# The last modulation row of a mixture-of-experts layer: from the experts' loop to the final sums

## The chip, the cores and the metric

One Trainium2 core runs the whole program. The time is in device microseconds; lower is better. The kernel before took 1674.91 us, the median of three runs (1671.81 to 1677.38). The core's engines work side by side and each takes its instructions in order: TensorE (PE; PEld is its weight load), VectorE (DVE), ScalarE (ACT), GpSimd (POOL), and SyncE (SP), which here only issues transfers.

## The reference

One layer of a diffusion trunk: modulated normalisation, three kinds of attention, an output projection, then a mixture of experts. The change lies in the last two lines of the layer and in the final normalisation.

```python
def hybrid_layer(...):
    mod = (c_act @ w_mod + b_mod).reshape(B_, 6, 1, D)
    ...
    h2 = rms_norm(x, g2) * (1 + mod[:, 4]) + mod[:, 3]
    ...
    f = hier_moe(h2.reshape(-1, D), w_rg, b_rg, w_re, b_re, w_up, w_down)
    x = x + mod[:, 5] * f.reshape(B_, S, D)
    return x, xc

def hier_moe(h, ...):            # top-1 group of 4, top-2 of its 8 experts: 32 experts
    gate = jax.nn.softmax(top_v, axis=-1) * p_grp
    ...
    def expert_block(args):
        g, u = jnp.split(xb @ w_up[e], 2, axis=-1)
        return (jax.nn.silu(g) * u) @ w_down[e]
    y = y[dest] * gate.reshape(-1)[order][:, None].astype(h.dtype)
    return jax.ops.segment_sum(y, tok_sorted, num_segments=n_tok)

def reference(...):
    return rms_norm(x, final_g)
```

There are 1024 tokens of width 1024, all in fp32. Each token goes to two experts; its two results are weighted by two gates, summed, multiplied by the modulation row `mod[5]` (one value for each column, the same for all tokens) and added to `x`.

## The kernel before

The first 940 us (modulation, projections, attention, output projection, routing) are the same in both kernels. Then comes a loop over the 32 experts, written out in full, with 128 places (partitions) for the tokens of each. Tokens beyond 128 for an expert go to overflow blocks in a loop whose count is read from the data (line 1985); in the profiled execution it has no turn.

**The experts' loop.** The weights come in tiles of 128 rows by 1024 columns, eight for an expert's `w_up` and four for its `w_down`, in one stream of 384 (lines 1881 to 1901). They lie in a ring of 34 buffers (`wraw`); SyncE issues the load of tile j + 34 when tile j is split. To multiply in fp32 precision with a faster format, each tile is split in two parts (line 1828): ScalarE rounds it to `whi`, VectorE subtracts to get the remainder `wlo` (line 1832). There are three buffers of each. The tokens are split in the same way into `xh`, `xl`, and the hidden activations into `ah`, `al`. For each tile TensorE does six matmuls of 512 columns (lines 1857 to 1859): high by high, high by low, low by high, for two halves of the columns. The order on the engines is the order in which the code is written (a manual schedule): the `w_up` tiles of expert e + 1 stand ahead of the `w_down` tiles of expert e, and the transposes of tokens and activations are set into the stream.

When the fourth `w_down` tile of an expert is done, `e_scatter` (line 1871) takes the result `py` from PSUM: ScalarE copies it to `y`, GpSimd multiplies `y` by `m5`, the modulation row spread over all partitions (line 1877), and GpSimd issues an indirect transfer that writes the 128 rows to the DRAM table `YS` (line 1878), at row `j * T + token` for choice j. For the last expert alone VectorE does copy and multiplication in one instruction (line 1874). During some seven experts, from (b, k) = (8, 0) on, the overflow tables are built by many small VectorE instructions, one of them behind each step of the stream.

**Behind the loop.** Each of the eight token tiles (128 tokens by 1024) needs its `x` (kept in DRAM as `X1`, loaded into the ring: four by GpSimd behind the scatter of expert 29, four and the final gain `fg` by SyncE), and the two rows of `YS`, `y0` and `y1`, 16 loads of 512 KB issued by SyncE once all scatters have landed. `FINAL` (line 58) is a string that sets the order of the steps `f_step` (line 2016): `s` does x + gate0 y0 + gate1 y1 in two VectorE instructions, `t` gives the first product to ScalarE and the first addition to GpSimd; both end with a ScalarE pass that squares and sums each row. `r` is a chain of small VectorE instructions for 1/sqrt; `o` scales by that and by `fg` on VectorE, `u` does so on ScalarE and GpSimd; both store the tile. This part is ordered by a scheduler that starts from the written order.

Of the kernel before, what the change touches and what calls it, by code (L numbers as in the profile page):

```python
# [8 lines left out]
F32 = mybir.dt.float32  # L9
# [3 lines left out]
AF = mybir.ActivationFunctionType  # L13
OP = mybir.AluOpType
# [4 lines left out]
D = 1024  # L19
# [27 lines left out]
DRAIN = 30  # L47
LATE = 3
HL = 1
XE = 4  # L50
START = """
Lx.0.4 Lm.0 Lx.4.8 R.0 Lm.1 Lw q.3 q.2 q.1 C.0 q.0 x.0.4 w q.5 q.6 q.7 q.4 h.0.0 x.4.8 a.0.0
R.1 h.1.0 Lx.8.10 C.1 q.9 h.2.0 h.3.1 Lm.2 R.2 q.8 h.0.1 h.1.1 x.8.10 Lm.3 C.2 h.2.1 h.3.0 a.1.0 a.0.1 h.1.2
# [1 line left out]
S.3.2 a.4.0 h.6.0 a.5.0 h.7.0 a.4.2 a.1.2 h.7.1 a.2.2 a.6.0 a.7.0 h.6.2 h.5.2 a.6.1 h.7.2 S.3.3 S.3.6 S.3.5 a.3.2 a.7.1  # L55
a.5.1 a.5.2 N a.7.2 a.6.2 S.3.7 a.0.2
"""
FINAL = "t2 s0 s1 r01 o0 t3 o1 r23 t4 t5 o2 r45 t7 t6 o4 u5 r6 r7 o7 o3 o6"
LAST = """
s0.30 T0.28 table.3 m.29 s1.30 x1.30 T4.28 p2.5 T8.28 T0.29 x0.30 v.28 s0.31 T4.29 s1.31 m.30 x0.31 T8.29 router.4  # L60
choose.4 p3.5 mixt.6 v.29 norm2.5 T0.30 T8.30 x1.31 m.31 T4.30 v.30 p0.6 na.7 rank.4 T0.31 T4.31 T8.31 h0.5 h1.5 p1.6
# [6 lines left out]
def body(nc, tc, d, tap=None, upto=None):  # L68
# [7 lines left out]
    def dmab(t, src):  # L76
        nc.sync.dma_start(t, src)  # L77
# [1174 lines left out]
    def ring():  # L1252
        rws.append(rws.pop(0))
        return rws[-1].tile([128, D], F32, name="wraw")
# [616 lines left out]
    def e_scatter(py, si_, last=False):  # L1871
        y = e2.tile([128, D], F32, name="y", bufs=2)
        if last:
            nc.vector.tensor_mul(y, py, m5)
        else:
            nc.scalar.copy(y, py)  # L1876
            nc.gpsimd.tensor_mul(y, y, m5)  # L1877
        return nc.gpsimd.indirect_dma_start(out=YS, out_offset=bass.IndirectOffsetOnAxis(ap=si_, axis=0),
                                            in_=y, in_offset=None, bounds_check=2 * T - 1, oob_is_err=False)

# [19 lines left out]
                load_tile(j + RW)  # L1900


    xts = []

    def load_ends():

        for t in range(XE):
            load_x1(t, nc.gpsimd)

    def load_x1(t, eng):  # L1910
        x2 = ring()
        rws.pop()
        eng.dma_start(x2, X1[t * 128:(t + 1) * 128, :])
        xts.append(x2)

    with tc.manual_schedule(engines={ET.PE, ET.DVE, ET.Activation, ET.Pool}):
# [29 lines left out]
        for j, (b, k) in enumerate(stream):  # L1946
# [20 lines left out]
            if kind == 1 and k == 3:  # L1967
                i_ = e_scatter(ps, sU[:, e:e + 1], e == E - 1)
                for p_ in scat:
                    tc.declare_no_dep(i_.ins, p_.ins, reason="rows of other tokens or choices")  # L1970
                scat.append(i_)
                if e == E - 3:
                    load_ends()
        for _ in side_work:
            pass

    for t in range(XE, NT):
        load_x1(t, nc.sync)
    fg = ring()
    rws.pop()  # L1980
    dmab(fg, bcast_rows(d["final_g"], D))


    nov = nc.values_load(novt[0:1, 0:1], min_val=0, max_val=NOV)
# [27 lines left out]
            dmab(yts[t][j], YS[j * T + t * 128:j * T + (t + 1) * 128, :])  # L2012
    s3 = e2.tile([128, NT], F32, name="s3", bufs=1)
    r3 = e2.tile([128, 2, NT], F32, name="r3", bufs=1)

    def f_step(what, ts):
        t = ts[0]
        xt, y0, y1 = xts[t], *yts[t]
        a, b = ts[0], ts[-1] + 1
        if what == "s":  # L2020
            nc.vector.scalar_tensor_tensor(xt, y0, gate[:, 0, t:t + 1], xt, op0=OP.mult, op1=OP.add)  # L2021
        elif what == "t":
            nc.scalar.activation(y0, y0, AF.Copy, scale=gate[:, 0, t:t + 1])  # L2023
            nc.gpsimd.tensor_add(xt, xt, y0)  # L2024
        if what in "st":
            nc.vector.scalar_tensor_tensor(xt, y1, gate[:, 1, t:t + 1], xt, op0=OP.mult, op1=OP.add)  # L2026
            nc.scalar.activation(y0, xt, AF.Square, accum_out=s3[:, t:t + 1])  # L2027
        elif what == "r":
            nc.vector.tensor_scalar(s3[:, a:b], s3[:, a:b], 1.0 / D, EPS, op0=OP.mult, op1=OP.add)  # L2029
            rsqrt(s3[:, a:b], r3[:, 0, a:b], r3[:, 1, a:b])  # L2030
        elif what == "o":
            nc.vector.scalar_tensor_tensor(xt, xt, r3[:, 0, t:t + 1], fg, op0=OP.mult, op1=OP.mult)  # L2032
        elif what == "u":
            nc.scalar.activation(xt, xt, AF.Copy, scale=r3[:, 0, t:t + 1])
            nc.gpsimd.tensor_mul(xt, xt, fg)
        if what in "ou":
            nc.sync.dma_start(d["out"][t * 128:(t + 1) * 128, :], xt)
# [129 lines left out]
```

## Time and profile before

| what | us |
|---|---|
| median of three runs | 1674.91 |
| the profiled execution, its own time | 1675.7 |
| its span, first to last instruction | 1673.9 |
| first scatter of the loop | at 992.73 |
| last scatter of the loop | at 1615.27 |
| first load of `YS` issued | at 1619.42 |
| last VectorE instruction ends | at 1668.70 |
| PE, DVE, ACT, POOL busy over the span | 1462.1, 1233.5, 999.1, 546.2 |

In a timeline row stand the start, the time, the engine, the line, the operation, what it writes and reads, how many such instructions in a row were put together, and in brackets how long the engine had stood still before it and what ended that. In a row of windows stand the stretch, its length, the busy time of PE, PEld, DVE, ACT and POOL with their instruction counts, the granted clock of TensorE (1 is full speed), the busy share of the 16 DMA engines, and what they moved in GB/s. A wait row names who waited, for whom, the total, how often, and the longest.

### The profile page before, as it was taken

What the parts mean: (1) busy time and instruction counts of PE and PEld (TensorE: products, weight loads), DVE (VectorE), ACT (ScalarE), POOL (GpSimd) and SP (SyncE); (2) the same over time, 40 slices, a digit from 0 to 9 for tenths busy, and PEclk for the clock granted to TensorE, in tenths of its full rate; (3) what the DMA queues carried; (4) which work ended last, traced back from release to release, by engine and by line L of the source; (5) the groups of instructions that cost most, each with busy time, mean ns of one, the idle gap of its engine ahead of it and who ended that gap; (6) DMA issues with size and microseconds to landing.
All of it is one profiled execution on the core that took longest, in us unless ns stands there. A gap on an engine that the chain in (4) does not pass through costs nothing. (4 is left out here: it accounts for less than half of the span.)

```text
span 1673.9 us, 24624 instructions
## 1 busy us (share of the span) xinstructions
PE 1462.1 (87%) x8611; PEld 1193.7 (71%) x8611; DVE 1233.5 (74%) x1936; ACT 999.1 (60%) x1602; POOL 546.2 (33%) x608
## 2 busy tenths in 40 slices
PE   6899799899989897999998689988999999999840
PEld 2698677777777776899998567666777777777730
DVE  5713657965544365867787689998999999999957
ACT  4624546754434523767664377766777777777742
POOL 0201423222322203377885413322222223233224
PEclk9999899999988897999999799999999999999975
DMA  9324572106543686222227789887999999999344
GB/s 325 102 58 137 163 227 67 49 27 186 128 109 96 200 268 244 77 65 89 64 89 273 274 302 337 317 306 261 335 349 344 342 343 344 339 347 340 144 179 192
DMA packets 163502, 353.18 MB, mean 211 GB/s; under 512 B 28247, under 2 KB 83735, under 8 KB 163376
## 3 DMA queue, kind: packets, MB, share of 16 engines
q1 hardware_dynamic: 139552, 307.87, 53.4%
q0 software_dynamic: 22096, 37.94, 7.4%
q10 hardware_dynamic: 1728, 5.78, 0.9%
q8 instruction: 69, 1.13, 0.3%
q14 instruction: 57, 0.47, 0.1%
HBM read 318.30 MB, written 49.30 MB: 220 GB/s over the span
## 5 line engine op out<-in xcount | busy, mean ns | idle before, releaser
L1832 DVE TENSOR_TENSOR wlo<-wraw,whi 128x1024 fp32r<-128x1024 f32 x384 | 505.8, 1338 | 42.8 <-ACT whi L1831 37.7
L1831 ACT CAST whi<-wraw 128x1024 fp32r<-128x1024 f32 x384 | 399.5, 1049 | 160.7 <-PE epu L1859 110.3
L1858 PE MATMUL epu<-wlo,xh 128*128 128x512 f32 x512 | 210.4, 411 | 44.0 <-DVE wlo L1832 42.7
L1857 PE MATMUL epu<-whi,xh 128*128 128x512 f32 x512 | 208.4, 407 | 2.2 <-ACT xh L1849 2.2
L1859 PE MATMUL epu<-whi,xl 128*128 128x512 f32 x512 | 203.9, 398 | 1.0 <-DVE xl L1850 1.0
L1858 PEld LDWEIGHTS epu<-wlo,xh 128*128 128x128 f32 x512 | 97.1, 190 | 89.5 <-DVE wlo L1832 69.3
L1836 POOL DMA_INDIRECT xg<-H,gidx x30 | 42.2, 1407 | 332.2 <-PE ept L1847 320.6
L1877 POOL TENSOR_TENSOR y<-y,m 128x1024 f32<-128x1024 f32 x31 | 88.8, 2865 | 136.2 <-ACT y L1876 136.2
L1273 DVE TENSOR_REDUCE nm<-S 128x1 f32<-128x1280 f32 x64 | 94.9, 1489 | 51.0 <-PE S L1272 42.4
L385 PE MATMUL pj<-wh,hh 128*128 128x256 f32 (+1 forms) x384 | 114.8, 299 | 1.3 <-ACT kbT L342 1.3
L1857 PEld LDWEIGHTS epu<-whi,xh 128*128 128x128 f32 x512 | 97.4, 190 | 24.0 <-ACT xh L1849 2.8
L387 PE MATMUL pj<-wh,hl 128*128 128x256 f32 (+1 forms) x384 | 113.3, 295 | 0.0
L386 PE MATMUL pj<-wl,hh 128*128 128x256 f32 (+1 forms) x384 | 113.3, 295 | 0.0
L1859 PEld LDWEIGHTS epu<-whi,xl 128*128 128x128 f32 x512 | 97.3, 190 | 22.3 <-DVE xl L1850 1.7
L1857 PE MATMUL epy<-whi,ah 128*128 128x512 f32 x256 | 109.0, 426 | 2.3 <-ACT y L1876 2.3
L1858 PE MATMUL epy<-wlo,ah 128*128 128x512 f32 x256 | 102.9, 402 | 0.7 <-DVE wlo L1832 0.7
L1859 PE MATMUL epy<-whi,al 128*128 128x512 f32 x256 | 102.3, 400 | 0.0
L374 PE MATMUL pj<-hh,wh 128*128 128x512 f32 (+1 forms) x240 | 99.9, 416 | 0.0
L1278 ACT ACTIVATE p<-S,nm 128x1280 f32<-128x1280 f32 x64 | 84.6, 1331 | 21.2 <-DMA x1t<-w_out 15.4
L375 PE MATMUL pj<-hl,wh 128*128 128x512 f32 (+1 forms) x240 | 92.1, 384 | 0.0
L376 PE MATMUL pj<-hh,wl 128*128 128x512 f32 (+1 forms) x240 | 91.9, 383 | 0.0
L1271 PE MATMUL S<-ak,aq 128*128 128x512 f32 (+1 forms) x192 | 76.1, 397 | 10.8 <-ACT p L1278 10.0
(447 smaller groups left out, 3513.6 us busy)
## 6 DMA issues: line engine op xcount, KB each, us to landing
wraw<-w_up SPq DMA_DIRECT2D x254, 512.0 KB
wraw<-w_down SPq DMA_DIRECT2D x127, 512.0 KB
wm<-w_mod SPq DMA_DIRECT2D x32, 512.0 KB
raw<-w_in SPq DMA_DIRECT2D x22, 512.0 KB
wm<-w_mod SPq DMA_DIRECT2D x32, 256.0 KB
aq<-QS SPq DMA_DIRECT2D x64, 128.0 KB
wraw<-YS SPq DMA_DIRECT2D x16, 512.0 KB
ak<-KS SPq DMA_DIRECT2D x8, 640.0 KB
```

What stands on the lines that cost most here:

```text
L374: nc.tensor.matmul(ps[:, :n], lhsT=a, rhs=x, start=(k == 0), stop=False)
L375: nc.tensor.matmul(ps[:, :n], lhsT=a, rhs=y, start=False, stop=False)
L376: nc.tensor.matmul(ps[:, :n], lhsT=b, rhs=x, start=False, stop=(k == 7))
L385: nc.tensor.matmul(ps[:, :n], lhsT=a, rhs=wh[:, k, :], start=(k == 0), stop=False)
L386: nc.tensor.matmul(ps[:, :n], lhsT=a, rhs=wl[:, k, :], start=False, stop=False)
L387: nc.tensor.matmul(ps[:, :n], lhsT=b, rhs=wh[:, k, :], start=False, stop=(k == 7))
L1273: V.tensor_reduce(u.nm[:, m:m + 1], sv, axis=AX.X, op=OP.max, negate=True)
L1831: nc.scalar.copy(hi, raw)
L1832: nc.vector.tensor_sub(lo, raw, hi.bitcast(F32))
L1857: nc.tensor.matmul(ps[:, cs], lhsT=ah[:, k, :], rhs=hi[:, cs], start=(k == 0), stop=False)
L1858: nc.tensor.matmul(ps[:, cs], lhsT=ah[:, k, :], rhs=lo[:, cs], start=False, stop=False)
L1859: nc.tensor.matmul(ps[:, cs], lhsT=al[:, k, :], rhs=hi[:, cs], start=False, stop=(k == nk - 1))
```

## The change

1. In the loop, `y` is scattered as it is: the GpSimd multiplication by `m5` is gone. For the last expert ScalarE and VectorE each copy one half.
2. The rows of `X1` are all loaded by GpSimd: `fg` and four of them behind the scatter of expert 29, four behind that of expert 30. SyncE loads none of them.
3. ScalarE makes 16 diagonal matrices of 128 by 128 (`gate_diagonals`): the identity scaled by the gates of one token tile and one choice, between its other work during experts 30 and 31. They lie in two buffers of the ring.
4. Behind the loop, a new step `p`: TensorE multiplies the diagonals by `y0` and `y1` and sums them in PSUM, four plain fp32 matmuls of 512 columns for each tile, in the two PSUM buffers of the loop's `epu`. The step `s` then multiplies that by `m5` and adds it to `x`, both on VectorE. The step `t` is gone. The last tile (`h`) does so in two halves. `u` is kept for one tile.

```diff
-FINAL = "t2 s0 s1 r01 o0 t3 o1 r23 t4 t5 o2 r45 t7 t6 o4 u5 r6 r7 o7 o3 o6"
+FINAL = "p0 p1 s0 p2 s1 r01 o0 p3 s2 o1 p4 s3 r23 o2 p5 s4 o3 p6 s5 r45 u4 p7 s6 o5 r6 h7 r7 o6 o7"
...
         if last:
-            nc.vector.tensor_mul(y, py, m5)
+            nc.scalar.copy(y[:, 0:512], py[:, 0:512])
+            nc.vector.tensor_copy(y[:, 512:], py[:, 512:])
         else:
             nc.scalar.copy(y, py)
-            nc.gpsimd.tensor_mul(y, y, m5)
...
+    def load_ends(e):
+
+        if e == E - 3:
+            fgs.append(kept())
+            nc.gpsimd.dma_start(fgs[0], bcast_rows(d["final_g"], D))
+        for t in range(4) if e == E - 3 else range(4, NT):
+            load_x1(t, nc.gpsimd)
+
+    def gate_diagonals():
+
+        for j in range(2):
+            dgs.append(kept().rearrange("p (t q) -> p t q", t=NT))
+            for t in range(NT):
+                nc.scalar.activation(dgs[j][:, t, :], ident, AF.Copy, scale=gate[:, j, t:t + 1])
+                yield
...
+                if e in (E - 3, E - 2):
+                    load_ends(e)
                 if e == E - 3:
-                    load_ends()
+                    side_work = gate_diagonals()
...
-    for t in range(XE, NT):
-        load_x1(t, nc.sync)
-    fg = ring()
-    rws.pop()
-    dmab(fg, bcast_rows(d["final_g"], D))
+    fg = fgs[0]
...
-        if what == "s":
-            nc.vector.scalar_tensor_tensor(xt, y0, gate[:, 0, t:t + 1], xt, op0=OP.mult, op1=OP.add)
-        elif what == "t":
-            nc.scalar.activation(y0, y0, AF.Copy, scale=gate[:, 0, t:t + 1])
-            nc.gpsimd.tensor_add(xt, xt, y0)
-        if what in "st":
-            nc.vector.scalar_tensor_tensor(xt, y1, gate[:, 1, t:t + 1], xt, op0=OP.mult, op1=OP.add)
+        if what == "p":
+            ps = pss[t] = pe.tile([128, D], F32, name="epu")
+            for n in range(2):
+                cs = slice(512 * n, 512 * n + 512)
+                for j, y in enumerate((y0, y1)):
+                    nc.tensor.matmul(ps[:, cs], lhsT=dgs[j][:, t, :], rhs=y[:, cs], start=(j == 0), stop=(j == 1))
+        elif what == "s":
+            nc.vector.tensor_mul(y0, pss[t], m5)
+            nc.vector.tensor_add(xt, xt, y0)
             nc.scalar.activation(y0, xt, AF.Square, accum_out=s3[:, t:t + 1])
+        elif what == "h":
+            for n in range(2):
+                cs = slice(512 * n, 512 * n + 512)
+                nc.vector.tensor_mul(y0[:, cs], pss[t][:, cs], m5[:, cs])
+                nc.vector.tensor_add(xt[:, cs], xt[:, cs], y0[:, cs])
+                nc.scalar.activation(y0[:, cs], xt[:, cs], AF.Square, accum_out=sh[:, n:n + 1])
+            nc.vector.tensor_add(s3[:, t:t + 1], sh[:, 0:1], sh[:, 1:2])
```

The following lists show the order in which instructions stand on an engine. GpSimd at the end of the loop, before (`y` is the block's result, `m_9600` the modulation row, `YS` the table in DRAM, `X_68` the table `X1`; line 1877 is the multiplication, 1878 the scatter, 1913 the load of `X1`):

```order
L1877 TENSOR_TENSOR y<-y,m_9600 128x1024
L1878 DMA YS<-y,sidx 2048x1024
L1877 TENSOR_TENSOR y<-y,m_9600 128x1024
L1878 DMA YS<-y,sidx 2048x1024
L1913 DMA wraw<-X_68 128x1024 x4
L1877 TENSOR_TENSOR y<-y,m_9600 128x1024
L1878 DMA YS<-y,sidx 2048x1024 x2
```

GpSimd at the same place in the changed kernel (line 1877 is now the scatter, 1914 the load of the final gain, 1928 that of `X1`, 1835 the gather of an expert's tokens):

```order
L1835 DMA xg_9601<-H_67,gidx 128x1024
L1877 DMA YS<-y,sidx 2048x1024 x3
L1914 DMA wraw<-final_g 128x1024
L1928 DMA wraw<-X_68 128x1024 x4
L1877 DMA YS<-y,sidx 2048x1024
L1928 DMA wraw<-X_68 128x1024 x4
L1877 DMA YS<-y,sidx 2048x1024
```

No multiplication stands ahead of a scatter any more, and four loads have come between the last two scatters.

VectorE at the start of the part behind the loop, before (lines 2021 and 2026 are the two products with additions, the other lines the first 1/sqrt chain, of which `r` and `s` are the small tiles, and line 2032 the scaling):

```order
L2021 SCALAR_TENSOR_TENSOR wraw<-wraw,gate 128x1024
L2026 SCALAR_TENSOR_TENSOR wraw<-wraw,gate 128x1024
L2021 SCALAR_TENSOR_TENSOR wraw<-wraw,gate 128x1024
L2026 SCALAR_TENSOR_TENSOR wraw<-wraw,gate 128x1024
L2029 TENSOR_SCALAR s_15891<-s_15891 128x2
L99 TENSOR_SCALAR r_15892<-s_15891 128x2
L101 TENSOR_TENSOR r_15892<-r_15892 128x2
```

VectorE at the same place in the changed kernel (line 2042 multiplies the sum in PSUM, `epu`, by the modulation row, line 2043 adds it to `x`):

```order
L2042 TENSOR_TENSOR wraw<-epu,m_9600 128x1024
L2043 TENSOR_TENSOR wraw<-wraw 128x1024
L2042 TENSOR_TENSOR wraw<-epu,m_9600 128x1024
L2043 TENSOR_TENSOR wraw<-wraw 128x1024
L2042 TENSOR_TENSOR wraw<-epu,m_9600 128x1024
L2053 TENSOR_SCALAR s_15878<-s_15878 128x2
L2043 TENSOR_TENSOR wraw<-wraw 128x1024
L98 TENSOR_SCALAR r_15879<-s_15878 128x2
```

The first VectorE instruction now reads what TensorE summed, and the first chain begins behind the multiplication of the third tile.

More of the change, by code (lines that the diff above doesn't have):

```diff
@@ L49 @@
 HL = 1
-XE = 4
 START = """
@@ L1900, in split_next, with kept, load_x1 @@
                 load_tile(j + RW)
[L1903 to L1910, printed above, removed]
+    xts, dgs, fgs = [], [], []
+    def kept():
         x2 = ring()
         rws.pop()
+        return x2
+    def load_ends(e):
[10 more added lines that the diff above has]
+                yield
+    def load_x1(t, eng):
+        x2 = kept()
         eng.dma_start(x2, X1[t * 128:(t + 1) * 128, :])
@@ L2014, in body @@
     r3 = e2.tile([128, 2, NT], F32, name="r3", bufs=1)
+    sh = e2.tile([128, 2], F32, name="sh", bufs=1)
+    pss = {}
     def f_step(what, ts):
```

## The prediction

> **What bounds the kernel now.** I read the page first, then the windows of the experts' loop, then who waits for whom, then the timeline of one expert, and last the timeline behind the loop.
>
> ```profile
> span 1673.9 us, 24624 instructions
> L1877 POOL TENSOR_TENSOR y<-y,m 128x1024 f32<-128x1024 f32 x31 | 88.8, 2865 | 136.2 <-ACT y L1876 136.2
> ...
> 1210.00:1510.00 300.00, 278.87 (x1261) 218.01 (x1261) 284.49 (x256) 228.72 (x255) 90.07 (x46) 1.00 0.94 343
> ...
> PE epu L1858 <- DVE wlo L1832: 26.8, 19, 1.4
> ...
> L1894 SPq DMA_DIRECT2D wraw<-w_down x127: 327/328/1081, 905.8 to 1552.2; - x127
> ```
>
> The stretch in the third line (columns: length, then busy time of PE, PEld, DVE, ACT and POOL, the granted clock, the DMA engines' share, GB/s) holds 15 experts of 20 us. For each, DVE is busy 19.0 us and PE 18.6 (its pipelined records overlap), ACT 15.2, POOL 6. The fourth line matters most: between 1200 and 1580 us PE waited 19 times, once per expert, 1.4 us each, for the low half of a split weight (`wlo`, line 1832), which VectorE makes. The weights are not late: the last one is issued at 1552.2 us, and the loop's second last scatter comes at 1609.22 (a row below), so the ring of 34 tiles is full. The timeline of one expert says why `wlo` is late:
>
> ```profile
> 1304.12 2.35 DVE L1832 TENSOR_TENSOR wlo<-wraw,whi 128x1024 fp32r<-128x1024 f32 x2
> 1305.02 0.40 PE L1857 MATMUL epu<-whi,xh 128*128 128x512 f32 x1
> 1305.38 0.50 PE L1858 MATMUL epu<-wlo,xh 128*128 128x512 f32 x1
> 1305.88 2.84 POOL L1877 TENSOR_TENSOR y<-y,m 128x1024 f32<-128x1024 f32 x1 [3.12 <-ACT y L1876]
> ...
> 1306.77 3.03 DVE L1832 TENSOR_TENSOR wlo<-wraw,whi 128x1024 fp32r<-128x1024 f32 x1 [0.31 <-ACT whi L1831]
> ...
> 1308.06 0.40 PE L1857 MATMUL epu<-whi,xh 128*128 128x512 f32 x1
> 1309.00 1.71 POOL L1878 DMA_INDIRECT YS<-y,sidx  x1 [0.28 <-POOL y L1877]
> 1309.86 0.50 PE L1858 MATMUL epu<-wlo,xh 128*128 128x512 f32 x1 [1.40 <-DVE wlo L1832]
> 1310.19 0.39 PE L1859 MATMUL epu<-whi,xl 128*128 128x512 f32 x1
> 1310.42 0.40 PE L1857 MATMUL epu<-whi,xh 128*128 128x512 f32 x1
> ```
>
> A split usually costs 2.35/2 = 1.18 us. The one that begins while GpSimd multiplies `y` by the modulation row lasts 3.03 us, and ends about one split behind the end of the multiplication (1305.88 + 2.84 = 1308.72; 1306.77 + 3.03 = 1309.80). So VectorE stands while GpSimd runs, and PE then waits. PE's starts are 0.23 us apart when nothing is late (1310.19 to 1310.42); from 1308.06 to 1309.86 there are 1.80, so the step loses **1.57 us**. A second, small loss stands before it: 1305.02 to 1305.38, 0.13 us too many, when GpSimd had not begun; VectorE is a little behind there by itself.
>
> **The change, part by part.**
>
> *The multiplication out of the loop.* All 31 GpSimd multiplications go. With 1.57 us less, an expert takes 20.00 - 1.57 = 18.43 us. What is late next? VectorE has 12 splits of 1.18, three of 0.68 (`xl`, `al`) and two of 0.69 (`sg`): 17.6 us, under 18.43 and close. ScalarE, with 15.2 us, is further off. So I let the whole 1.57 go. Bounds: the wait alone (1.40), or both losses (1.70). How many experts? The scatters behind the multiplication mark them:
>
> ```profile
> 992.73 1.72 POOL L1878 DMA_INDIRECT YS<-y,sidx  x1 [0.29 <-POOL y L1877]
> 1032.74 1.70 POOL L1878 DMA_INDIRECT YS<-y,sidx  x1 [0.28 <-POOL y L1877]
> 1189.01 1.70 POOL L1878 DMA_INDIRECT YS<-y,sidx  x1 [0.28 <-POOL y L1877]
> 1609.22 1.03 POOL L1878 DMA_INDIRECT YS<-y,sidx  x1 [0.28 <-POOL y L1877]
> ```
>
> 2 periods of 20.0 up to 1032.74 and 21 more from 1189.01 to 1609.22: **23 x 1.57 = 36.1 us saved** (32.2 to 39.1). Between lie 7 periods, 156.3 us, in which the overflow tables are built by small VectorE instructions in the loop. There the multiplication holds up whatever VectorE has next:
>
> ```profile
> 1050.77 2.36 DVE L1715 TENSOR_TENSOR dd<-gmx 128x8 f32<-128x8 f32 x1
> 1058.63 0.16 DVE L1724 TENSOR_TENSOR gate<-ds,pg 128x8 f32<-128x8 f32 x1
> 1145.04 0.50 PE L1858 MATMUL epu<-wlo,xh 128*128 128x512 f32 x1 [1.01 <-DVE wlo L1832]
> ```
>
> VectorE loses 2.36 - 0.16 = 2.2 us there; where other waits cover part of it, PE shows 1.0. I take the middle, **7 x 1.5 = 10.5 us saved** (7 to 15).
>
> *The last scatters.* The last block's result is copied by two engines in halves instead of one multiplication:
>
> ```profile
> 1318.18 0.68 DVE L1864 TENSOR_TENSOR sg<-sg,epu 128x512 f32<-128x512 f32 x1
> 1613.77 1.22 DVE L1874 TENSOR_TENSOR y<-epy,m 128x1024 f32<-128x1024 f32 x1 [2.08 <-PEq L1985]
> 1590.76 2.22 POOL L1913 DMA_DIRECT2D wraw<-X  x4
> wraw<-X POOLq DMA_DIRECT2D x4, 512.0 KB, 6.1
> ...
> 1629.65 1.13 ACT L2023 ACTIVATE wraw<-wraw,gate 128x1024 f32<-128x1024 f32 x1
> ```
>
> 1.22 becomes about 0.68: 0.5 us saved on the path. Against it, four loads of `X1` now stand on GpSimd's queue between the last two scatters: 2.22 us of issue, 6.1 to landing. Scatter E-2 leaves about 2.8 us sooner (no multiplication), so the loads are issued well before the last scatter, but their last bytes can still be under way beside it: 0 to 1.5 us, I take 0.5. The sum is 0. The load of the final gain and the first four `X1` tiles are 20 us earlier and hidden by the last experts; so are the 16 diagonals on ScalarE, which is busy 15.2 us of 20. If that cover were gone they would cost at most 16 x 0.3 = 5 us, a quarter of the 1.13 us that the same operation takes on 1024 columns.
>
> *Behind the loop.* Before, VectorE runs from the first landed tile to the last scaled one:
>
> ```profile
> 1622.92 1.28 DVE L2021 SCALAR_TENSOR_TENSOR wraw<-wraw,gate 128x1024 f32<-128x1024 f32 x1 [7.93 <-DMA wraw<-YS]
> 1630.19 0.16 DVE L101 TENSOR_TENSOR r<-r 128x2 f32<-128x2 f32 x1
> 1630.38 0.16 DVE L103 SCALAR_TENSOR_TENSOR r<-r,s 128x2 f32<-128x2 f32 x1
> 1643.30 3.43 DVE L2026 SCALAR_TENSOR_TENSOR wraw<-wraw,gate 128x1024 f32<-128x1024 f32 x1 [2.28 <-POOL wraw L2024]
> 1666.22 2.48 DVE L2032 SCALAR_TENSOR_TENSOR wraw<-wraw,r 128x1024 f32<-128x1024 f32 x2
> 35.56 7.03 PE L233 MATMUL pt<-wm,cact 128*2 128x512 f32 x16
> 1606.40:1609.10 2.70, 2.69 (x6) 2.15 (x7) 0.30 (x1) 0.00 (x0) 2.50 (x1) 0.50 0.00 0
> 1609.10:1613.00 3.90, 3.90 (x17) 3.14 (x16) 1.23 (x1) 1.05 (x1) 1.03 (x1) 0.95 0.21 79
> 1616.00:1623.00 7.00, 0.00 (x0) 0.00 (x0) 0.08 (x1) 0.00 (x0) 0.27 (x1) 0.52 0.45 160
> ```
>
> That is 1622.92 to 1668.70, 45.8 us. Now each tile needs four plain fp32 matmuls of 512 columns. The nearest row is line 233: 8 such matmuls (two records each) in 7.03 us, 0.88 each, 3.5 us a tile at full clock. But PE has been idle, and the granted clock is about a half (0.52); a burst after a pause ran 2.7 us at 0.50 before it rose. So the first tile's sum takes about 5.2 us, during which VectorE now has nothing to do. Then VectorE sets the pace: 7 x (1.22 from PSUM + 1.18 add) = 16.8, the halved tile 4 x 0.68 = 2.7, seven scalings of 1.24 = 8.7, and five chains of 11 small instructions at 0.2 = 11. The six GpSimd additions that held up VectorE (3.43 against 1.28) are gone; one GpSimd multiplication stays, 2 us. Sum 41.2, plus 2 us waiting for the sums of tiles 1 and 2 (3.5 apart, VectorE needs 2.4). 5.2 + 41.2 + 2 = 48.4, so **2.6 us lost** (-3 if the first sum hides and no lock falls badly; +8 if the sums pace it at reduced clock for a while).
>
> Sum: against this execution's 1675.7 us (1673.9 and 1.8 around the span), -36.1 - 10.5 + 0 + 2.6 gives 1631.7. The median shown is 1674.91, 0.8 below, so I forecast **1631**.
>
> One thing could speak against more work behind GpSimd's queue:
>
> ```profile
> 1301.27 1.49 POOL L1836 DMA_INDIRECT xg<-H,gidx  x1 [10.56 <-PE ept L1847]
> 1301.78 0.68 DVE L1850 TENSOR_TENSOR xl<-ept,xh 128x512 fp32r<-128x512 f32 x1
> ```
>
> A gather of 1.49 us and a VectorE instruction of its usual 0.68 lie beside each other, and neither waits, so I add nothing. The Trainium skill (SBUF — State Buffer, section "SBUF: two separate sides") says that descriptors of DMAs issued from GpSimd are written over the port pair that it shares with VectorE, and that VectorE's work can hold them up. [...]
>
> **Rivals.**
>
> *The weight stream becomes the bound.* An expert moves 343 GB/s x 20 us = 6.86 MB; at 18.43 us that is 372 GB/s.
>
> ```profile
> 1490.00:1510.00 20.00, 18.60 (x85) 14.55 (x85) 18.97 (x18) 15.25 (x17) 6.05 (x4) 1.00 0.99 364
> 1625.00:1630.00 5.00, 0.00 (x0) 0.00 (x0) 3.41 (x5) 2.55 (x5) 0.00 (x0) 0.50 1.02 406
> ```
>
> The highest 20 us stretch shows 364 GB/s at a share of 0.99, which would give 6.86/0.364 = 18.85 us per expert, 30 x 0.42 = 13 us back: 1644. Against it: the reads behind the loop run at 406, and the ring's lead of 34 tiles (some 50 us) pays a deficit of 13 us without a wait. Chance 0.07. The Trainium skill (DMA: Bandwidth & Descriptors, Specifications) gives about 358 GB/s as a core's share of HBM; by that an expert would take 19.2 us and the total, with the lead of no use, an estimated 1654. The 406 above does not agree with it as a limit.
>
> *The clock never rises behind the loop.* With PE pausing between tiles, it stays at half: 3.5 becomes 3.5/0.55 = 6.4 us, eight tiles 51 us, and then the last tile's 6 (two halves 1.4, a ScalarE pass 1.1, a chain 2.2, the scaling 1.2): 57 instead of 48.4, 1640. The 2.7 us row speaks for a quick rise. Chance 0.08. The Trainium skill (TensorE: Matmul & The Clock Gate, section "A second HAM failure mode: psum-queue depth-cycling") describes such small pauses re-throttling the array.
>
> *The wait moves.* VectorE is so nearly full (17.6 of 18.4) that half of the 1.57 comes back as waits elsewhere in the expert: 46.6/2 back, 1655. Chance 0.08.
>
> *The multiplication is not the cause.* Were the scatter or ScalarE's copy what stretches VectorE, the loop would stay at 20 us and the end cost 2.6: 1677, no change. Against: instructions of any kind stretch exactly inside the multiplication, and the scatter at 1309.00 begins when the split is nearly done. Chance 0.04. That the row stays in the loop by mistake can't be: no multiplication is left on GpSimd's list there.
>
> *Slower: the fp32 sums.* They are on the path of the end with nothing to hide behind. It decides if one of the 32 matmuls costs over (45.8 + 46.6 + 5 - 6)/32 = 2.9 us (the 6 as above, the 5 what can be told from no change); at 3.2 us the end is 32 x 3.2 + 6 = 108 us and the total 1675.7 - 46.6 + 62 = 1691. Line 233's 0.88 and 1.6 at half clock speak against it. Chance 0.03.
>
> **How the numbers follow.** Forecast 0.70, by its own bounds 1618 (39.1 + 15 saved, end -3) to 1646 (32.2 + 7 saved, 1.5 and +8 lost). With the stream and the clock, both inside, 0.85 lies between 1617 and 1647. A measurement here tells 0.3%, 5 us, from no change. Faster: 0.70 + 0.07 + 0.08 + 0.08 = 0.93; same 0.04; slower 0.03.
>
> **What would show it.** Right: scatters 18.4 us apart, every split in the loop about 1.2 us, PE's wait of 1.4 us gone; behind the loop, VectorE from the first landed tile to the last scaling in some 48 us, tile sums 3.5 us apart from the second on. Wrong: ScalarE or VectorE waiting for `wraw` (the stream), sums 6.4 us apart (the clock), new waits of PE for `wlo` at another step, or splits still 3 us long beside the scatter.

## The result, and the profile after

The changed kernel takes **1624.09 us** (median of four runs, 1623.25 to 1624.32), the kernel before 1675.06 beside it (four runs, 1671.81 to 1677.38): ratio **0.970** (95% interval 0.969 to 0.972). I had forecast 1631. The profiled execution has a span of 1622.5 us, 51.4 less than before.

First the page: the span and the group of VectorE's weight splits (busy us, mean ns of one), then the windows of the loop (length, busy time of PE, PEld, DVE, ACT and POOL, granted clock, DMA share, GB/s), then the waits from 1200 to 1530 us (total, times, longest):

```profile
span 1622.5 us, 24721 instructions
...
L1831 DVE TENSOR_TENSOR wlo<-wraw,whi 128x1024 fp32r<-128x1024 f32 x384 | 463.1, 1221 | 43.6 <-ACT whi L1830 40.9
```

```profile
1210.00:1510.00 300.00, 300.00 (x1377) 239.37 (x1377) 282.62 (x278) 249.71 (x278) 43.85 (x33) 1.00 0.99 376
```

```profile
PEld epu L1857 <- DVE wlo L1831: 6.9, 18, 0.4
```

TensorE's records now cover the whole stretch, 300 us of 300. The row for PE's wait for `wlo`, 19 times 1.4 us before, is gone; only its weight loads still wait, 18 times and at most 0.4 us each, for the most part beneath running products. No row has an engine waiting for `wraw`, though the transfers go at 376 GB/s at a share of 0.99: the stream is fast enough. The same place of the loop, in the timeline of one expert:

```profile
1300.61 1.27 POOL L1877 DMA_INDIRECT YS<-y,sidx  x1 [3.32 <-ACT y L1876]
...
1301.32 2.37 DVE L1831 TENSOR_TENSOR wlo<-wraw,whi 128x1024 fp32r<-128x1024 f32 x2 [0.33 <-ACT whi L1830]
...
1303.53 0.39 PE L1857 MATMUL epu<-wlo,xh 128*128 128x512 f32 x1
1303.76 0.39 PE L1858 MATMUL epu<-whi,xl 128*128 128x512 f32 x1
```

The scatter stands alone on GpSimd; the split beside it takes its usual 1.18 us (two in 2.37), and the products follow each other in steps of 0.23. The scatters that mark the expert periods:

```profile
993.02 1.29 POOL L1877 DMA_INDIRECT YS<-y,sidx  x1 [3.34 <-ACT y L1876]
1172.39 1.28 POOL L1877 DMA_INDIRECT YS<-y,sidx  x1 [3.31 <-ACT y L1876]
1538.81 1.25 POOL L1877 DMA_INDIRECT YS<-y,sidx  x1 [17.05 <-ACT y L1876]
1558.09 1.01 POOL L1877 DMA_INDIRECT YS<-y,sidx  x1 [15.29 <-ACT y L1876]
1559.10 2.16 POOL L1928 DMA_DIRECT2D wraw<-X  x4
1565.36 1.01 POOL L1877 DMA_INDIRECT YS<-y,sidx  x1 [4.09 <-DVEq L1998]
```

From 1172.39 to 1538.81 are 20 periods of 18.32 us, against 20.0 before. Behind the loop: first the windows, then the timeline.

```profile
1574.00:1577.00 3.00, 2.73 (x4) 1.13 (x5) 0.00 (x0) 0.00 (x0) 0.00 (x0) 0.50 1.01 374
...
1580.00:1584.00 4.00, 4.00 (x10) 1.71 (x9) 2.45 (x2) 0.44 (x1) 0.00 (x0) 0.96 1.02 418
```

```profile
1574.27 30.90 PE L2040 MATMUL epu<-wraw 128*128 128x512 f32 x64 [10.54 <-DMA wraw<-YS]
1580.98 1.23 DVE L2042 TENSOR_TENSOR wraw<-epu,m 128x1024 f32<-128x1024 f32 x1 [15.91 <-PE epu L2040]
1584.42 1.23 DVE L2042 TENSOR_TENSOR wraw<-epu,m 128x1024 f32<-128x1024 f32 x1 [0.95 <-PE epu L2040]
...
1611.99 0.15 DVE L102 SCALAR_TENSOR_TENSOR r<-r,s 128x1 f32<-128x1 f32 x1
1612.06 0.15 DVE L2051 TENSOR_TENSOR s<-sh 128x1 f32<-128x1 f32 x1
...
1612.37 2.37 POOL L2059 TENSOR_TENSOR wraw<-wraw 128x1024 f32<-128x1024 f32 x1 [46.00 <-DVE r L103]
1612.56 2.19 DVE L102 SCALAR_TENSOR_TENSOR r<-r,s 128x1 f32<-128x1 f32 x1
...
1617.53 1.28 DVE L2056 SCALAR_TENSOR_TENSOR wraw<-wraw,r 128x1024 f32<-128x1024 f32 x1
```

The first sum needs 6.71 us from the landing to VectorE's start, almost all of it at half clock (0.50; 0.96 from 1580 on); the next ones come 3.44 apart. Then VectorE runs to 1618.81.

Where the 51.4 us went, from the two timelines (us):

| stretch | before | after | difference |
|---|---|---|---|
| span's start to the first `up` product | 950.23 | 952.32 | +2.1 |
| to the end of the last product of the loop | 663.45 | 611.41 | -52.0 |
| to the first `YS` load issued | 5.74 | 6.94 | +1.2 |
| to its landing | 3.50 | 3.60 | +0.1 |
| to the end of the last scaling | 45.78 | 44.54 | -1.2 |
| to the span's end | 5.20 | 3.69 | -1.5 |

The first row is code that the change doesn't touch; over the profiles of this study it lies between 947.7 and 954.5. So a difference below some 5 us is read from the stretches of a trace, not from two medians.

### The profile page after: what moved, and what is told of

Same layout as the page of the kernel before. It is cut to its first block, busy times and chain, and to the rows that moved or that the text cites. A ratio compares the mean times of both kernels' runs of the same rounds, so it can differ in the third digit from the quotient of the medians.

```text
span 1622.5 us, 24721 instructions
## 1 busy us (share of the span) xinstructions
PE 1483.1 (91%) x8675; PEld 1206.7 (74%) x8675; DVE 1176.1 (72%) x1945; ACT 998.7 (62%) x1615; POOL 432.8 (27%) x576
## 4 chain that ended last, share of the span: by engine, by line
PE 65%; DVE 15%; DMA 8%; ACT 6%; issue 4%; POOL 1%; SPq 0%; DVEq 0%; POOLq 0%; ACTq 0%
PE epu L1857 7%; PE epu L1858 7%; PE epu L1856 7%; DMA wm<-w_mod 4%; PE epy L1856 3%; PE epy L1857 3%; PE epy L1858 3%; PE apt L1297 3%; PE ept L1846 2%; PE pj L373 2%; PE cps L958 2%; PE apt L1291 2%; PE S L1270 2%; PE pj L384 2%; PE S L1271 1%
## 5 line engine op out<-in xcount | busy, mean ns | idle before, releaser
L1831 DVE TENSOR_TENSOR wlo<-wraw,whi 128x1024 fp32r<-128x1024 f32 x384 | 463.1, 1221 | 43.6 <-ACT whi L1830 40.9
L1292 ACT COPY eT<-apt 128x512 f32<-128x512 f32 (+1 forms) x96 | 46.5, 515 | 62.5 <-PE apt L1291 60.6
```

Source lines behind the costliest of these rows:

```text
L1831: nc.vector.tensor_sub(lo, raw, hi.bitcast(F32))
```

## The experiments

### What the multiplication costs the loop

Theory: GpSimd's multiplication holds VectorE's split of two SBUF tiles, and that alone makes the wait. Rivals: VectorE's fullness (the wait moves), the weight stream, the scatter or the copy. Four kernels, timed together (the kernel before took 1675.19 us there), and a fifth in a later batch.

**A multiplication that nobody needs**, in the changed kernel, behind each scatter but the last; `junk` is a tile of its own:

```diff
+        i_ = nc.gpsimd.indirect_dma_start(out=YS, ...)
+        if not last:
+            nc.gpsimd.tensor_mul(junk[:, :1024], m5[:, :1024], m5[:, :1024])
+        return i_
```

> The changed kernel with one GpSimd multiplication of 128x1024 added behind each of the 31 scatters in the loop; it reads the modulation row twice and writes a tile that nothing reads, so no instruction waits for its result. If a GpSimd multiplication by itself holds up VectorE, experts are 19.6 to 20.1 us apart again, PE waits about 1.4 us per expert for the low half of a weight, and the time is 1660 to 1676. If the old kernel lost its time through what waited for the product (the scatter and the buffer y), nothing changes: 18.3 us per expert, 1624.

Measured: **1688.54 us** (ratio 1.007, 1.004 to 1.009), more than forecast: with the multiplication behind the scatter the kernel is slower than before. The timeline of one expert:

```profile
1312.81 5.85 DVE L1832 TENSOR_TENSOR wlo<-wraw,whi 128x1024 fp32r<-128x1024 f32 x3 [0.32 <-ACT whi L1831]
1313.38 1.92 POOL L1881 TENSOR_TENSOR junk<-m 128x1024 f32<-128x1024 f32 x1
```

Its waits (1230 to 1530 us, 15 experts):

```profile
PE epu L1858 <- DVE wlo L1832: 29.5, 15, 2.0
```

Three splits take 5.85 us instead of 3.5. The longest is 3.60: from 1312.81 to 1316.4, which is 1.1 behind the multiplication's end at 1315.30. In the kernel before, the held split also ends 1.1 us behind the multiplication (1309.80 against 1308.72). Here it begins 0.57 us earlier than the multiplication's record does, and is held longer, so PE's wait is 2.0 instead of 1.4. Why a split that is already under way is held was not found out; spans on GpSimd are rough.

**The same with half the columns** (512 instead of 1024):

> The same with 512 columns instead of 1024. If the time that VectorE stands is the length of the GpSimd instruction, the stretched split is about 1.2 us shorter than with the full one (1.8 instead of 3.0) and, since VectorE has 0.7 us to spare per expert, less than half of the loss returns: 18.4 to 18.9 us per expert, 1627 to 1643. If each GpSimd instruction costs a fixed stop whatever its length, the same as the full one: 1660 or more. If it is the waiting for the product: 1624.

Measured: **1658.82 us** (ratio 0.991, 0.989 to 0.993), again above the forecast. The multiplication is 0.86 us shorter, and so are the split and PE's wait (1.1 us), by 0.9:

```profile
1296.32 5.01 DVE L1832 TENSOR_TENSOR wlo<-wraw,whi 128x1024 fp32r<-128x1024 f32 x3 [0.30 <-ACT whi L1831]
1296.90 1.06 POOL L1881 TENSOR_TENSOR junk<-m 128x512 f32<-128x512 f32 x1
```

The periods are 20.56, 19.70 and 18.32 us with 1.92, 1.06 and no multiplication: from 1.06 on, each microsecond of it costs one. That is the dose that the theory asks for; the sizes that I expected were too small because I took the split to begin later than the multiplication.

**The kernel before without the multiplication** (its one line in the loop is taken out; `mod[5]` is then applied to the last expert's rows alone, so this kernel leaves out a part of the computation):

> The kernel before, with the GpSimd multiplication left out of the loop and nothing in its place: the modulation row is applied to the last expert's rows alone. Everything behind the loop is as before. If the loop alone brings the gain and the new end is worth about nothing (VectorE from the first landed tile to its last scaling 1.2 us shorter, the last transfer 1.5 us shorter, the last scatter 1.2 us later), it takes 1624 to 1628. If the new end carried part of the gain by itself, it takes 1632 or more; if the new end costs, as I forecast with 2.6 us, 1621.

Measured: **1621.14 us** (ratio 0.969, 0.967 to 0.970). The scatters, with the old code behind the loop, stand as in the changed kernel:

```profile
1296.24 1.27 POOL L1877 DMA_INDIRECT YS<-y,sidx  x1 [3.32 <-ACT y L1876]
1314.55 1.28 POOL L1877 DMA_INDIRECT YS<-y,sidx  x1 [2.80 <-ACT y L1876]
```

18.31 us. So the missing multiplication alone explains the loop; the diagonals, the order of loads and the new end add nothing to it. By my own expectation 1621 was the sign of an end that costs 2.6 us, but the traces show no such cost: from the last product to the end of the span this kernel takes 59.9 us, the changed one 58.8. The new end, which does the work that is left out here, costs no more than the old one. The 3.7 us between the two spans (1618.8 and 1622.5) lie ahead of it: 1.6 in the code ahead of the loop, and 3.2 from the first `up` product to the last product (608.2 us against 611.4), a stretch that takes 608.6 to 611.4 us in the five other traces of the end's section that have the changed kernel's loop. The changed kernel's end gives 1.1 of it back.

**The multiplication on VectorE**, straight from PSUM, for every expert of the kernel before:

```diff
-        if last:
-            nc.vector.tensor_mul(y, py, m5)
-        else:
-            nc.scalar.copy(y, py)
-            nc.gpsimd.tensor_mul(y, y, m5)
+        nc.vector.tensor_mul(y, py, m5)
```

> The kernel before, with the multiplication in the loop done by VectorE straight from PSUM for every expert (as for the last one), instead of ScalarE's copy and GpSimd's multiplication. The result is the same. It puts 1.2 us more work per expert on VectorE, which has some 17.5 of 18.3 us filled. If what counts is that VectorE is held up for 1.8 us and not who works, experts are 18.6 to 19.3 us apart and the time is 1633 to 1655: part of the gain without the new end. If VectorE can be filled up to PE's pace, 18.3 us and 1625. If its place in VectorE's order is bad (PE waits for the low half as before), 20 us and 1670.

Measured: **1644.18 us** (ratio 0.982, 0.980 to 0.983), as expected; its timeline:

```profile
1311.95 1.22 DVE L1873 TENSOR_TENSOR y<-epy,m 128x1024 f32<-128x1024 f32 x1
1313.09 3.49 DVE L1832 TENSOR_TENSOR wlo<-wraw,whi 128x1024 fp32r<-128x1024 f32 x3
```

VectorE does 1.22 us more of its own for each expert, no split is longer than 1.23, and the period is 18.93 us: 0.6 of the 1.22 is lost. That answers the rival of a full VectorE: it has some 0.6 us to give, and being held for 1.85 us costs 1.7. The same multiplication costs 0.6 us on VectorE and 1.7 on GpSimd, which is off the path.

**Other kinds of instruction on GpSimd**, in the changed kernel, in turn:

```diff
+            if len(scat) % 2:
+                nc.gpsimd.memset(junk, 2.0)
+            else:
+                nc.gpsimd.tensor_scalar(junk[:, :512], m5[:, :512], 2.0, None, op0=OP.mult)
```

> The changed kernel with an extra GpSimd instruction behind each scatter, as in the two runs with an extra multiplication, but of two other kinds in turn: behind every other expert's a product of m5's first 512 columns with a constant (one tile read), behind the others a fill of 128x1024 with a constant (nothing read). Theory A, what holds VectorE's split of two SBUF tiles is GpSimd reading SBUF: the periods with the product of one tile are longer than 18.33 us (19.5 or so, as with the half multiplication's 19.70, if it takes about 1 us), those with the fill stay at 18.33. Theory B, any GpSimd instruction that writes SBUF holds it: both kinds are longer. Theory C, only one that reads two tiles: both stay at 18.33. By A the time is about 1624 + 15 x 1.2 = 1642, by B 1655 or more, by C 1624.

Measured: **1623.11 us** (the kernel before 1671.96 beside it; ratio 0.971, 0.967 to 0.975). The timeline, two experts:

```profile
1188.79 1.27 POOL L1878 DMA_INDIRECT YS<-y,sidx  x1 [3.31 <-ACT y L1877]
1190.08 2.37 POOL L1884 TENSOR_SCALAR junk<-m 128x512 f32<-128x512 f32 x1
1207.36 1.27 POOL L1878 DMA_INDIRECT YS<-y,sidx  x1 [3.26 <-ACT y L1877]
1208.63 0.97 POOL L1882 MEMSET junk<- 128x1024 f32 x1
1225.68 1.28 POOL L1878 DMA_INDIRECT YS<-y,sidx  x1 [3.31 <-ACT y L1877]
```

The period with the fill is 18.32 us, that with the product of one tile 18.57, although this takes 2.37 us. The two splits beside it take up to 1.63 us, 0.4 too long, and it is GpSimd's instruction that seems to wait: its shortest record is 1.53 us, its median 2.37. So theory C comes nearest, and A falls: that GpSimd reads SBUF is not enough. In this loop only the multiplication of two tiles held VectorE for its whole length. Why the two forms differ stays open. The Trainium skill (SBUF — State Buffer, section "SBUF: two separate sides") gives the rule that a VectorE instruction with two SBUF inputs and a GpSimd instruction that reads SBUF share a port pair, which goes whole to whichever starts first. The loop's multiplication agrees with it; the product of one tile (periods 0.25 us longer, not 1.5) does not, nor does the split of the run with the extra multiplication that, by its record, began first and was held.

### What the end costs

Four edits of the end, one by one, in one batch (before: 1674.06 us, 11 runs). The medians, 1618.67 to 1626.31, lie 7.6 us apart; the executions of the changed kernel itself, in two batches with medians of 1624.09 and, below, 1619.84, lie 8.9 apart (1617.12 to 1626.01). So no median here decides about an edit; the traces do, one execution of each.

**Products that keep the clock up** (ten of 128x512 into a PSUM tile that nobody reads, ahead of the sums):

```diff
+    warm = pe.tile([128, 4, 128], F32, name="ept").rearrange("p a b -> p (a b)")
+    for _ in range(10):
+        nc.tensor.matmul(warm, lhsT=ident, rhs=m5[:, 0:512], start=True, stop=True)
```

> The changed kernel with ten more products of 128x512 on TensorE, of the identity with m5 into a PSUM tile that nobody reads, behind the loop and ahead of the sums. They wait for nothing, so they fill the first 8.6 us (10 x 2 records of 0.43) of the 10.5 us in which TensorE waits for the YS rows. Theory: the first sum takes 6.7 us from the landing to VectorE's start because the granted clock is 0.50 there; with the clock up it takes about 8 x 0.43 = 3.4 to 4, and the time falls by 2.5 to 3.3 us, to 1621 to 1621.6. Rival: the first sum is bound by its second load or by weight loads, not by the clock: unchanged within 0.5 us of 1624.1. If the products run over the landing, the gain shrinks.

Measured: **1626.31 us** (ratio 0.971, 0.969 to 0.974); no gain. The timeline, and the window of its second half:

```profile
1566.04 11.32 PE L2028 MATMUL ept<-m,ident 128*128 128x512 f32 x20 [6.15 <-issue]
1577.20 5.31 PE L2043 MATMUL epu<-wraw 128*128 128x512 f32 x12
...
1580.84 1.23 DVE L2045 TENSOR_TENSOR wraw<-epu,m 128x1024 f32<-128x1024 f32 x1 [19.59 <-DMA wraw<-YS]
```

```profile
1571.00:1577.00 6.00, 6.00 (x15) 2.66 (x14) 0.00 (x0) 0.00 (x0) 0.00 (x0) 1.00 1.02 386
```

TensorE begins them only 6.15 us behind its last product. The bracket names nothing that it waited for ("issue"), and I had expected that they wait for nothing. But TensorE's instruction queue (`PEldq`) does wait, at the statement of the overflow loop, line 1998. The first row counts its waits for semaphores (how many, shortest, median and longest in ns, start of the first and the last), the second is one of them alone:

```profile
L1998 PEldq EVENT_SEMAPHORE  x13: 51/51/2577, 1559.9 to 1565.7; - x13
...
L1998 PEldq EVENT_SEMAPHORE  x1: 1492/1492/1492, 1563.3 to 1563.3; - x1
```

The wait of 1.49 us ends at 1564.81, when the last scatter has landed (issued at 1561.53 and landed 3.25 us later by the chain of waits: 1564.78); eight short waits and the branch take most of the rest. So in this program no product behind the loop begins before the last scatter has landed; products that are to keep the clock up would have to stand ahead of the loop's statement, which was not tried. When they begin, the clock is down. The ten products take 11.3 us instead of the 8.6 that they need at full clock, which they reach by 1571, and run some 8 us past the landing. But the first sum then takes 3.64 us (1577.20 to 1580.84) instead of 6.71. The rows had long landed here, so a wait for the second row could also have gone; but in the changed kernel TensorE is busy from the first product on (2.73 of the 3.00 us from 1574.00, at 0.50). So the clock is what makes it slow, as the theory said; my filling was too long and started too late.

**The last `X1` loads from SyncE** instead of GpSimd:

```diff
-            load_x1(t, nc.gpsimd)
+            load_x1(t, nc.gpsimd if e == E - 3 else nc.sync)
```

> The changed kernel with the second four loads of X1 issued by SyncE instead of GpSimd, whose queue of issues has been empty since 1507 us. Theory: the last scatter lands 4.59 us after its issue instead of 3.22 because those four loads, issued 6.3 us ahead of it, still move beside it; from SyncE they go out before the last expert's end, the scatter lands in 3.2 to 3.4 us, and the time falls by 1.0 to 1.4 us, to 1622.7 to 1623.1. Rival: the scatter itself is slower for another reason (its rows come from a copy on two engines): landing stays at 4.6 and the time at 1624.1.

Measured: **1621.38 us** (ratio 0.967, 0.965 to 0.970). In its chain of waits the last scatter lands in 3.23 us; in that of the changed kernel, where it was issued at 1565.36, it took 4.59.

```profile
1564.06 3.23 DMA YS<-y,sidx
```

From the last product to the first `YS` load it takes 5.8 us instead of 6.94, the expected 1.1. But that is no proof that the edit gave it: in the repetition below, which has the loads on GpSimd, the same stretch takes 5.6 us. In both of these executions the last two scatters are 8.8 us apart, not 7.3, so the last one leaves later, and in the repetition it lands in 3.25 us although the loads stand ahead of it. By these traces the edit alone can gain only where the scatters come closer.

**The two half copies side by side** (the order between them taken out):

```diff
-            nc.scalar.copy(y[:, 0:512], py[:, 0:512])
-            nc.vector.tensor_copy(y[:, 512:], py[:, 512:])
+            c0 = nc.scalar.copy(y[:, 0:512], py[:, 0:512])
+            c1 = nc.vector.tensor_copy(y[:, 512:], py[:, 512:])
+            tc.declare_no_dep(c1.ins, c0.ins, reason="other columns")
```

> The changed kernel with the order between the two half copies of the last block's result taken out (they write different columns of one tile), so that ScalarE and VectorE copy side by side. Theory: the halves ran one after the other, 0.59 and 0.69 us with a gap, only because both write the tile y; now the two end 0.7 us behind the last product instead of 1.34, and the time falls by 0.5 to 0.65 us, to 1623.5. Rival: both engines read the same PSUM bank or are held by something else: no change.

Measured: **1620.82 us** (ratio 0.969, 0.967 to 0.972). First the timeline of the changed kernel, then this one's:

```profile
1563.76 0.59 ACT L1873 COPY y<-epy 128x512 f32<-128x512 f32 x1 [2.27 <-PE epy L1858]
1564.38 0.69 DVE L1874 COPY y<-epy 128x512 f32<-128x512 f32 x1 [2.51 <-ACT y L1873]
```

```profile
1560.59 0.58 ACT L1873 COPY y<-epy 128x512 f32<-128x512 f32 x1 [3.24 <-PE epy L1858]
1560.59 0.69 DVE L1874 COPY y<-epy 128x512 f32<-128x512 f32 x1 [2.88 <-PE epy L1858]
1562.05 1.01 POOL L1878 DMA_INDIRECT YS<-y,sidx  x1 [5.52 <-DVEq L1999]
```

The copies do run together and end 0.6 us sooner, but the scatter follows 0.77 us behind them instead of 0.29, so about 0.1 is left. What GpSimd waits for there was not found out.

**Tile 4 scaled on VectorE** (`u4` becomes `o4` in the order of the end):

> The changed kernel with tile 4's last scaling on VectorE like the others (1.24 us) instead of ScalarE and GpSimd. Theory: GpSimd's multiplication of 2.37 us holds a small instruction of VectorE for 2.19 us, and 2.19 - 0.1 - 1.24 = 0.8 us less stands on VectorE's chain: 1623.2 to 1623.4. Rival: VectorE has slack there (it waits for the next sum anyway): then the 1.24 us that are added stand in the chain too, and the time is 0 to 0.5 us longer.

Measured: **1618.67 us** (ratio 0.967, 0.964 to 0.969). From VectorE's first tile at 1576.16 to the end of the last scaling it takes 37.0 us, against 37.8 in the changed kernel (38.0 in the repetition): the 0.8 us expected. The one GpSimd multiplication that was left behind the loop held VectorE in the same way.

**The changed kernel again**, with the two that follow (before: 1675.16 us, 11 runs):

> The changed kernel once more, unchanged, beside the two that follow: 1622 to 1626 us. In its profile one thing is open: whether TensorE's clock falls to a half behind its 2.6 us wait for the next to last block's copy. In the profile of the changed kernel it did not, in three of the four variants looked at last it did, at 1.55 us more between the last two scatters (8.8 us instead of 7.3).

Measured: **1619.84 us** (ratio 0.968, 0.966 to 0.971). The clock did fall behind the wait for the copy, and the last two scatters are 8.81 us apart (7.27 in the first profile). The windows behind that wait show it best in the kernel with the half copies, which has the same loop, beside the first profile of the changed kernel:

```profile
1553.50:1557.50 4.00, 4.00 (x12) 3.14 (x11) 1.02 (x1) 1.94 (x4) 3.03 (x5) 0.57 0.50 145
```

```profile
1558.00:1563.00 5.00, 5.00 (x22) 4.04 (x23) 1.38 (x2) 2.04 (x5) 3.17 (x5) 1.00 0.51 164
```

12 products in 4 us against 22 in 5.

**The last block in a free PSUM buffer:**

```diff
-ps = (pe.tile(... name="epu"), None)[0] if kind == 0 else pd.tile(... name="epy")
+ps = pe.tile(... name="epu") if kind == 0 or b == len(blocks) - 1 else pd.tile(... name="epy")
```

> The changed kernel with the last block's product written to one of the two epu buffers, which are free by then, instead of the one epy buffer. Theory: TensorE waits 2.6 us ahead of the last block because the copy of the block before must empty epy (before the change 2.3 us; the diagonals on ScalarE add 0.3), and in some executions the clock falls to a half behind this wait: without it the last two scatters stand about 4.7 us apart instead of 7.3 (or 8.8), and the time falls by 2.3 to 3.5 us. Rival: TensorE waits for the last split of a weight tile as long anyway, and no more than 0.5 us goes.

Measured: **1619.20 us** (ratio 0.967, 0.965 to 0.969): no gain over the repetition. Its chain of waits:

```profile
1560.45 7.63 DMA YS<-y,sidx
```

The 2.6 us wait is gone, the scatters are 5.37 us apart, and the last one now lands in 7.63 us instead of 4.59 or 3.25: it leaves 4.4 us behind the first of the `X1` loads (1556.09) instead of 6.3 or more. The landing of the fourth load says the same. In its row the last number is the us from issue, here at 1557.71, to landing:

```profile
wraw<-X POOLq DMA_DIRECT2D x1, 512.0 KB, 9.1
```

In the changed kernel's first profile the fourth load was issued at 1560.72 and took 7.7. So these loads end at 1566.8 and 1568.5, and the scatters land 1.2 and 1.5 us behind them, at 1568.08 and 1569.95. In the seven other traces with these loads on GpSimd's queue between the last two scatters it is 0.2 to 1.7 us. So the 3.25 us of the repetition are not those of a scatter with nothing under way: its last load landed 1.7 us behind the scatter's issue. Neither theory said so: the gain is hidden behind transfers that the change itself put there.

**All edits of the end together**, with two products instead of ten:

> All edits of the end together: the last X1 loads from SyncE, the two half copies side by side, tile 4 scaled on VectorE, the last block in an epu buffer, and two products of 128x512 ahead of the sums (TensorE begins them 6.2 us behind the last product, so that two at half clock, 4 x 0.85 = 3.4 us, fit before the rows land; ten ran 8 us over). Each by what its own trace showed: -1.1, -0.1, -0.8, -2.6 and, with the clock rising 5.4 us behind the first product, -2 to -2.5 for the first sum. Sum: 6.6 to 7.1 us below the unchanged kernel beside it, about 1617. Rival: they lie beside each other (the clock falls anyway, the rows land no earlier), and the sum is below 4 us.

Measured: **1613.55 us** (ratio 0.963, 0.961 to 0.965), 6.3 below the repetition beside it, the fastest of all: both kernels are beaten. In the two traces the first `up` product stands at 951.29 and 951.30, so the spans, 1612.3 and 1618.0, can be compared: 5.7 us less. The timeline:

```profile
1553.63 1.01 POOL L1878 DMA_INDIRECT YS<-y,sidx  x1 [15.30 <-ACT y L1877]
...
1563.05 3.10 SPq L76 DMA_DIRECT2D wraw<-YS  x6
1571.44 1.23 DVE L2046 TENSOR_TENSOR wraw<-epu,m 128x1024 f32<-128x1024 f32 x1 [13.33 <-DMA wraw<-YS]
```

Of the 5.7, 3.35 lie between the next to last scatter and the first `YS` load (9.42 us against 12.77). With the loads moved alone it was 12.99, with the free buffer alone 13.71: the free buffer pays once the loads are out of its way. 1.5 are the first sum (8.39 us from the issue to VectorE against 9.87; I expected 2 to 2.5), and 1.0 is VectorE's end (37.0 against 38.0).

## Why the prediction was right, and where its sizes were off

| term | predicted | measured | 
|---|---|---|
| 23 plain expert periods | -36.1 | -37.9 |
| 7 periods with the overflow tables | -10.5 | -13.6 |
| last scatters (from the next to last one to the first load of `YS`) | 0 | +2.4 |
| from the first landing to the last scaling | +2.6 | -1.2 |
| what follows the last scaling | none | -1.5 |
| ahead of the first scatter (+0.3), landing of the first rows (+0.1) | none | +0.4 |
| sum | -44.0 | -51.4 |

**The cause holds.** I had read that VectorE stands while GpSimd multiplies and PE then waits. Taking out the multiplication alone gives the whole loop gain, putting one back takes it away, and its length sets the price. One sentence was too wide: that instructions of any kind stretch inside the multiplication. In one expert of the kernel before, whose multiplication has a record of 4.63 us (from 1070.95), a split of 1.20 us and two small instructions of 0.22 and 0.18 ran inside that record at their usual length; only the next split, from 1073.45, was held, for 3.22 us.

**The loop, 1.57 us for an expert, was a little small.** 1.68 went (20.00 to 18.32), next to my upper bound of 1.70, but not for the reason that this bound gave. The small loss ahead of the multiplication is still there: at that place the changed kernel has a step of 0.34 us instead of 0.23, where the kernel before had 0.36, and a second one of 0.34 behind it, as the kernel before had.

```profile
1299.58 0.40 PE L1856 MATMUL epu<-whi,xh 128*128 128x512 f32 x1
1299.92 0.50 PE L1857 MATMUL epu<-wlo,xh 128*128 128x512 f32 x1
```

What went beside the 1.57 is mostly the slow step right behind the wait, 1309.86 to 1310.19 in the prediction's rows, 0.33 us, of which I had counted nothing. For the seven table periods I took the middle, 1.5, between PE's 1.0 and VectorE's 2.2; they gave 1.94 (156.3 to 142.7 us). The instruction that was held 2.36 us takes 0.17 now:

```profile
1048.94 0.17 DVE L1714 TENSOR_TENSOR dd<-gmx 128x8 f32<-128x8 f32 x1
```

With VectorE this near to being the bound, its loss was the better guide than the one wait that I looked up.

**The last scatters, sized at nothing, cost 2.4 us** (10.20 to 12.58 from the next to last scatter to the first load of `YS`). Half of it is the distance from that scatter to the last product. The scatter leaves 2.6 us sooner, as forecast, and nothing behind it comes sooner for that; against it, the last block's products ran at full clock and took 1.4 us less than before, where the clock had fallen behind the wait for the copy (the prediction's row at 0.50). That was luck of this execution: in the repetition the clock fell. The other half lies behind the last product: the gain by half copies did not come (they ran one after the other, since both write `y`), and the `X1` loads took 1.4 of the 0 to 1.5 that I had allowed.

**The end, "2.6 us lost", gave 1.2 back.** The first sum was worse than my 5.2 (6.71, for the clock rose after some 6 us and not 2.7). The term that was mis-sized most is VectorE's 41.2: it ran from 1580.98 to 1618.81, 37.8 us, of which 1.9 were waits for sums as forecast, so 35.9. The chains are why. I charged 11 for 55 small instructions at 0.2 us; with the large instructions and the one that GpSimd holds taken off as charged (28.2 and 2), an estimate of some 6 is left for them. The 0.2 holds where each waits for the one before it; most are now woven between other instructions, and start 0.07 to 0.12 us apart (1611.99 and 1612.06 above).

**The last 1.5 us** I had left out: before, two scalings ended the span together; now there is one at a time, and the last output has less ahead of it. This was read from the traces only, and not tried.

**The rivals.** The stream is not the bound: 376 GB/s with no wait for a weight tile. So the figure of some 358 GB/s that the Trainium skill gives as a core's share (DMA: Bandwidth & Descriptors, Specifications) is no limit here, where one core runs alone, over 300 us and not only in a burst. The clock came up in time: tile sums 3.44 apart, not 6.4. Half of the gain did not come back elsewhere. The plain fp32 sums cost 0.86 us a product, far from the 2.9 at which the change would have lost.

## What to carry to other kernels

An engine with much idle time can still set the pace: ask not how busy it is, but which instruction of a tight engine gets longer while it works, and try the same work in another form or on the tight engine itself. When a wait near the end is taken away, look at what transfer the freed instruction then meets; an edit that is worth nothing alone can be worth 3 us with another. And price small instructions by whether they follow each other's results or can be woven in.

## What the runs showed of the hardware that was not expected

- GpSimd's product of two tiles held a VectorE split whose record begins 0.57 us before its own; its product of one tile with a constant, and a fill, held next to nothing (0.25 and 0 us a period).
- The clock of TensorE falls to a half behind a wait of 2.59 us in some executions and not in others of the same code, which is worth 1.55 us here.
- At a loop with a data-dependent count of zero, TensorE's queue waits for transfers of other engines that are still under way: in the run with ten products its first product behind the loop came 6.15 us behind the last one before it, 1.3 us behind the landing of the last scatter.
- An indirect scatter behind four loads of 512 KB on GpSimd's queue landed behind the last of them in all nine traces that have this order, by 0.2 to 1.7 us: 3.2 to 3.3 us from its own issue (as with no such loads) when it left 7.7 us or more behind the first load, 4.5 to 4.6 at 5.2 to 6.3, and 5.7 to 7.6 at 4.4 to 4.7.
